# Neighbourhood attention layer on one core: last pair split into an output operand, bias rows held once, weight tiles freed singly, last row scaled on two engines

## The chip, the cores and the metric

The kernel runs on one core of a Trainium2 chip. The metric is the device time in microseconds of one execution, taken as the median of several runs. The core has a matrix engine (TensorE, in the profile PE, with its weight loads as PEld), three engines for elementwise work (VectorE or DVE, ScalarE or ACT, GpSimd or POOL) and SyncE (SP), which here issues all the transfers between HBM and the on-chip memory SBUF. Products go to eight PSUM banks. Each engine runs its own instructions in order and waits for others through semaphores.

## The reference

One layer of an encoder: RMSNorm, one projection to q, k, v and a gate, two-dimensional neighbourhood attention (16 heads of 64, a grid of 32 rows by 64 columns, windows of 8 rows by 16 columns, a learned bias per head), a SiLU gate, an output projection with a residual, and a last RMSNorm. x is (1, 2048, 1024) in float32.

```python
def neighbourhood_mixer(h, w_in, rpb):
    proj = h @ w_in
    q, k, v, gate = jnp.split(proj, 4, axis=-1)
    o = neighbourhood_attention(heads(q), heads(k), heads(v), rpb)
    return o.reshape(B, S, D_INNER), gate
...
    s = jnp.einsum('bnqhd,bknjhd->bhnqkj', qr, kr) * scale
    s = jnp.where(col_valid, s + bias, NEG_INF)
    p = jax.nn.softmax(s, axis=-1)
    o = jnp.einsum('bhnqkj,bknjhd->bnqhd', p, vr)
...
h = rmsnorm(x, g)
o, gate = neighbourhood_mixer(h, w_in, rpb)
x = x + (o * jax.nn.silu(gate)) @ w_out
return rmsnorm(x, norm_f)
```

## The kernel before

Each float32 operand of a large product is split into two parts that the matrix engine takes at full rate, a high one (ACT rounds it) and a low one (DVE or POOL subtracts the high one from the value). A product of 128x128 by 128x512 is then three matmuls: high by high, high by low, low by high.

The program is written out by hand in one order per engine. Its main parts are these.

The start warms PE with ten matmuls of zeros (L780). `first_groups` (L417) then multiplies the first k weight tile by the first quarter of x as its pieces come in, `load_item` having issued all the loads on SP.

`projections` (L430) is a generator that yields after every matmul. It runs over 56 "halves", each a unit of q, k, v or gate for one quarter of the rows. `items` lists what has to be loaded and split, in order; `load_ahead` issues the loads (L151 for weights into tiles called raw), and `consume` calls `use_item`, which splits one item (L197 on ACT, L198 on DVE or POOL). `may_use` (L272) holds a weight item back while five weight tiles are live; a tile is live until the whole half that uses it last is done. `group` (L378) multiplies q, k and gate units, `group_v` (L394) V units. `evac` (L348) takes a product from PSUM, scales it by the row norms and writes q, k (split) and gate to scratch tensors in HBM.

The attention runs over 64 steps `pairs[i]`: two heads (a pair p of eight), a group T of eight grid rows (four of them, called row groups), and two of four column blocks C. For one step, `scores` multiplies (L549) and adds the bias tables em on DVE (L556) ahead of an exponential on ACT; `normalise` (L562) has the reciprocals on DVE and scales x on POOL (L567); `turns` transposes x through PE (L572) and copies it to pta on DVE and ACT (L596, L597); `values` multiplies by V (L617), and after the second step of a pair og is gated on DVE (L631) and stored to the scratch tensor ogd (L634). The bias tables of a pair come from its raw bias rows e (two tiles, L519): `bias` (L523) adds a mask, one on POOL and one on DVE for each column type. Pairs run p = 0 to 7 in row group 0, then six pairs in row groups 1, 2, 3 each, and the last two pairs interleaved.

The loop at L852 interleaves all this: for each step it feeds a fixed number of matmuls of `projections` (later of `outputs`) by a clock that counts them, with `normalise` and `turns` of the step before and `scores` of the step itself between them. `store(key, lag, f)` puts an action off by so many counts of that clock, and loads for the next step go the same way (`later_loads`).

`outputs` (L726) multiplies the 16 row tiles of 128 rows by the two halves of the output weights. `load_og` (L655) loads a row tile of ogd (512 KB, eight pairs) once all its pairs are stored, `split_og` (L665) splits it on ACT and DVE. `add_rows` adds the residual, `finish` (L692) computes the norm on DVE, scales the two halves of the row tile and sends them.

The lines that decide the waits in question:

```python
live = {tiles_(*i[1:]) for i in items[:state["used"]] if i[0] == "w" and last_use["w", i[1]] >= d}
return len(live | {tiles_(a, b)}) <= 5
...
ep = pool("ep", 4)
...
later_loads(load_qk(*nx), 5, 4)
if nx[0] != p:
    later_loads(load_e(nx[0]), 20, 3)
```

Of the kernel before, what the change touches and what calls it, by code (L numbers as in the profile page):

```python
# [67 lines left out]
def build(ctx, tc, x, xt, wg, rpb, w_out, n0, nf, masks, out):  # L68
# [25 lines left out]
    mp = pool("mp", 6)  # L94
    ep = pool("ep", 4)
    ev = pool("ev", 8)
# [33 lines left out]
    raws, wh, wl, asked_at = {}, {}, {}, {}  # L130
    woh, wol = {}, {}

    def load_item(it):
# [12 lines left out]
        asked_at[it] = clock[0]  # L146
        if kind in "xs":
            nc.sync.dma_start(t, xt[a * 128:(a + 1) * 128, b * 512:(b + 1) * 512])
        elif kind == "w":
            u = a[0]  # L150
            nc.sync.dma_start(t.rearrange("p (k c) -> p k c", c=256), wg[u, :, 2 * b:2 * b + 2, :])  # L151
        else:
            nc.sync.dma_start(t, w_out[a * 128:(a + 1) * 128, b * 512:(b + 1) * 512])
# [10 lines left out]
    def use_item(it):  # L164
# [7 lines left out]
        if kind == "x":  # L172
# [4 lines left out]
            if b < 2:  # L177
                raws["z", a, b] = t
        elif kind in "sz":
            square(a, t, b)  # L180
        elif kind == "w":
# [9 lines left out]
            else:  # L191
# [4 lines left out]
                h, l = wh[a, b // 2][:, s], wl[a, b // 2][:, s]  # L196
            nc.scalar.activation(h, t, AF.Copy)  # L197
            (nc.gpsimd if (b + u) % 2 and state["half"] > 0 else nc.vector).tensor_tensor(l, t, h.bitcast(F32), OP.subtract)  # L198
        else:
# [68 lines left out]
    AHEAD = 5  # L268
    clock = [0.0]
    state = dict(used=0, loaded=0, half=-1, done_halves=0, event=0.0)  # L270
# [107 lines left out]
    def group(w, a, c, n):  # L378
        p = bank(512, "pp")
        cols = slice(a * 128, a * 128 + 128)  # L380
        for k in range(NK):
# [7 lines left out]
            yield 1  # L389
            nc.tensor.matmul(p, wl[w, k // 4][:, k % 4, cols], hh[k, c], start=False, stop=(k == NK - 1))  # L390
            yield 1
        return p

    def group_v(w, t):  # L394
# [3 lines left out]
        for k in range(NK):  # L398
# [6 lines left out]
            yield 1  # L405
            nc.tensor.matmul(p, hl[k, c][:, o], h, start=False, stop=(k == NK - 1))  # L406
            yield 1
            if k in (2, 5):
# [8 lines left out]
    def first_groups(w):  # L417
        ps = [bank(512, "pp") for _ in range(2)]
        for k in range(NK):
            need(("x", k, 0))  # L420
            need(("w", w, k // 2))
            for a, p in enumerate(ps):
                cols = slice(a * 128, a * 128 + 128)
                h, l = wh[w, k // 4][:, k % 4, cols], wl[w, k // 4][:, k % 4, cols]
                nc.tensor.matmul(p, h, hh[k, 0], start=(k == 0), stop=False)
                nc.tensor.matmul(p, h, hl[k, 0], start=False, stop=False)
                nc.tensor.matmul(p, l, hh[k, 0], start=False, stop=(k == NK - 1))
        return ps

    def projections():  # L430
        for n, (kind, j, ph, c) in enumerate(halves):
# [10 lines left out]
            else:  # L442
                for a in range(2):
# [4 lines left out]
                    if n == len(halves) - 1:  # L448
# [3 lines left out]
                        else:  # L452
                            split_og(0)
                    if n >= 4:
# [15 lines left out]
    KT, VT, QT, EM, SG, E = {}, {}, {}, {}, {}, {}  # L470
    OG = {}
# [131 lines left out]
    def values(i):  # L603
# [25 lines left out]
        if cs[1] == 3:  # L629
# [3 lines left out]
            def keep():  # L633
                nc.sync.dma_start(ogd[T][:, :, p], og.rearrange("p (i q) -> p i q", i=4))  # L634
                written.add(("og", p, T))

            store(("og", p, T), 4, keep)

# [11 lines left out]
    tiles = S // 128  # L650

    def og_ready(n):
        return all(("og", p, n // 4) in written for p in range(NP))

    def load_og(n):  # L655
        T, i = divmod(n, 4)
        must(*[("og", p, T) for p in range(NP)])
        G[n] = t = wp([128, NK, 128], F32, "ograw")
        nc.sync.dma_start(t, ogd[T][:, i])

# [4 lines left out]
    def split_og(n):  # L665
# [3 lines left out]
        for j in range(2):  # L669
            s = slice(4 * j, 4 * j + 4)  # L670
            nc.scalar.activation(h[:, s], t[:, s], AF.Copy)  # L671
            nc.vector.tensor_tensor(l[:, s], t[:, s], h[:, s].bitcast(F32), OP.subtract)  # L672
        G[n] = (h, l)

    squared = [0]

    def add_rows(n, j, ps):
# [8 lines left out]
        def square():  # L686
            nc.scalar.activation(xr, y, AF.Square, scale=0.5 ** 0.5, accum_out=st[:, j:j + 1])
            squared[0] += 1

        store(("y", n, j), 5, square)  # L690

    def finish(n):  # L692
        y, st = Y.pop(n)
        h, r, a = st[:, 2:3], st[:, 3:4], st[:, 4:5]
# [9 lines left out]
        def scale():  # L704
            nc.vector.scalar_tensor_tensor(y[0], y[0], r, late["nf"][0], op0=OP.mult, op1=OP.mult)
            if n == tiles - 1:
                nc.vector.scalar_tensor_tensor(y[1], y[1], r, late["nf"][1], op0=OP.mult, op1=OP.mult)
            else:
                nc.scalar.activation(y[1], y[1], AF.Copy, scale=r)
# [16 lines left out]
    def outputs():  # L726
# [19 lines left out]
        for k, (n, j) in enumerate(turns_):  # L746
# [7 lines left out]
            gh, gl = G[n]  # L754
            p = bank(512, "po")
            for i in range(NK):
                while (i, j) not in woh:
                    consume(1, True)
                if k < 6 and i % 2 == 0:
                    consume(1)  # L760
                nc.tensor.matmul(p, gh[:, i], woh[i, j], start=(i == 0), stop=False)  # L761
                yield 1
                nc.tensor.matmul(p, gl[:, i], woh[i, j], start=False, stop=False)  # L763
                yield 1
                nc.tensor.matmul(p, gh[:, i], wol[i, j], start=False, stop=(i == NK - 1))  # L765
                yield 1
# [11 lines left out]
    zp = bank(512, "zp")  # L778
    for _ in range(10):
        nc.tensor.matmul(zp, z[:, :128], z, start=True, stop=True)  # L780
# [39 lines left out]
    def prepare(i):  # L820
# [85 lines left out]
```

## Time and profile before

| | us |
|---|---|
| median of three runs | 1155.54 (1155.35 to 1156.7) |
| the profiled execution | 1155.26 |
| its span, first to last instruction | 1153.5 |
| PE busy in the span | 1125.1 |
| mean granted clock of PE | 0.993 of full |
| HBM read and written | 155.91 MB and 67.11 MB |

The profile is one execution. Busy time of PE is the union of its matmuls, whose ends overlap: a matmul of 512 columns is listed with 0.39 us, but two follow each other at 0.227 us from start to start. What counts for PE is therefore the time from start to start. A row of the timeline gives start, duration, engine, line of the kernel, operation and tiles, and in brackets the idle time of that engine just before it with what ended it. "SPq" rows are the issuing of transfers by SP, not the transfers; a DMA row in the chain of waits is the time from the issue to the release of what waited.

### The profile page before, as it was taken

How to read it: one execution, taken by the hardware profiler on the slowest of the kernel's cores; microseconds unless marked ns; L12 is line 12 of the kernel's file. 1: busy time of each engine (PE TensorE's matmuls, PEld its weight loads, DVE VectorE, ACT ScalarE, POOL GpSimd, SP SyncE). 2: the span in 40 equal slices, each digit the busy share in tenths (PEclk: the TensorE clock that was granted, in tenths of full speed). 3: DMA queues.
4: the chain of work that ended last, by engine and by line, in shares of the span. 5: the costliest groups of instructions: out<-in, count | busy, mean ns of one | idle time of the engine just before them, and what ended most of it. 6: DMA issues, size and time to landing. Idle time of an engine off the chain costs nothing.

```text
span 1153.5 us, 21778 instructions
## 1 busy us (share of the span) xinstructions
PE 1125.1 (98%) x7858; PEld 916.4 (79%) x7858; DVE 572.6 (50%) x1453; ACT 467.5 (41%) x1190; POOL 383.7 (33%) x461
## 2 busy tenths in 40 slices
PE   8989999999999999999999999999999999999997
PEld 6868888888788888878887788888778777788875
DVE  6620554441244564126565455346555756566544
ACT  8222344232333444234444454344444544444322
POOL 1210442432232143314443544225533553233300
PEclk9999999999999999999999999999999999999999
DMA  7453867564554678457686787658877975865352
GB/s 244 126 160 109 270 213 219 162 225 110 154 183 145 214 222 240 118 165 195 224 245 198 207 250 222 208 163 230 235 230 210 281 230 188 255 194 189 104 174 73
DMA packets 139755, 224.45 MB, mean 195 GB/s; under 512 B 11776, under 2 KB 56320, under 8 KB 139648
## 3 DMA queue, kind: packets, MB, share of 16 engines
q1 hardware_dynamic: 139648, 223.06, 63.7%
q8 instruction: 62, 1.02, 0.4%
q14 instruction: 45, 0.37, 0.1%
HBM read 155.91 MB, written 67.11 MB: 193 GB/s over the span
## 4 chain that ended last, share of the span: by engine, by line
PE 58%; DMA 6%; DVE 3%; issue 3%; POOL 3%; ACT 1%; SPq 0%; DVEq 0%; POOLq 0%; ACTq 0%
PE pp L390 9%; PE pp L386 8%; PE pp L388 8%; PE o L617 6%; PE s L549 5%; PE po L763 4%; PE po L765 4%; PE po L761 4%; PE ph L572 3%; PE pv L404 3%; PE pv L402 3%; PE pv L406 3%; POOL x L567 1%; DMA ograw<-ogd 1%; DMA ogd<-og 1%
## 5 line engine op out<-in xcount | busy, mean ns | idle before, releaser
L390 PE MATMUL pp<-hh,wl 128*128 128x512 f32 x752 | 296.3, 394 | 2.0 <-POOL wl L198 2.0
L386 PE MATMUL pp<-hh,wh 128*128 128x512 f32 x752 | 295.3, 393 | 0.0
L388 PE MATMUL pp<-hl,wh 128*128 128x512 f32 x752 | 293.9, 391 | 0.0
L567 POOL TENSOR_SCALAR x<-x,st 128x360 f32<-128x360 f32 (+5 forms) x256 | 154.6, 623 | 250.7 <-DVE st L565 226.4
L559 ACT ACTIVATE x<-x,st 128x360 f32<-128x360 f32 (+5 forms) x256 | 151.8, 594 | 49.4 <-DVE st L556 49.3
L390 PEld LDWEIGHTS pp<-hh,wl 128*128 128x128 f32 x752 | 141.1, 188 | 33.4 <-POOL wl L198 2.9
L388 PEld LDWEIGHTS pp<-hl,wh 128*128 128x128 f32 x752 | 141.2, 188 | 30.5 <-issue 0.7
L386 PEld LDWEIGHTS pp<-hh,wh 128*128 128x128 f32 x752 | 141.2, 188 | 29.5 <-issue 0.5
L597 DVE COPY pta<-ph 128x384 f32<-128x384 f32 (+3 forms) x128 | 61.3, 516 | 165.8 <-PE ph L572 165.7
L198 POOL TENSOR_TENSOR wl<-raw,wh 128x512 fp32r<-128x512 f32 x60 | 83.3, 1393 | 161.6 <-ACT wh L197 155.2
L556 DVE CUSTOM_DVE_ANT_0 x<-s,em 128x360 f32<-128x360 f32 (+5 forms) x256 | 123.9, 539 | 7.3 <-PE s L549 5.3
L198 DVE TENSOR_TENSOR wl<-raw,wh 128x512 fp32r<-128x512 f32 x64 | 61.4, 969 | 93.9 <-ACT wh L197 92.6
L596 ACT ACTIVATE pta<-ph 96x256 f32<-96x256 f32 (+1 forms) x224 | 59.2, 333 | 118.7 <-PE ph L572 118.7
L402 PE MATMUL pv<-wh,hh 128*128 128x512 f32 x256 | 100.9, 394 | 3.5 <-ACT wh L197 3.5
L761 PE MATMUL po<-woh,gh 128*128 128x512 f32 x256 | 100.4, 392 | 2.1 <-ACT gh L671 2.0
L404 PE MATMUL pv<-wl,hh 128*128 128x512 f32 x256 | 101.4, 396 | 1.0 <-DVE wl L198 1.0
L763 PE MATMUL po<-woh,gl 128*128 128x512 f32 x256 | 100.4, 392 | 1.6 <-DVE gl L672 1.6
L765 PE MATMUL po<-wol,gh 128*128 128x512 f32 x256 | 100.9, 394 | 0.0
L406 PE MATMUL pv<-wh,hl 128*128 128x512 f32 x256 | 100.4, 392 | 0.0
L617 PEld LDWEIGHTS o<-pta,vt 96*64 96x64 f32 (+2 forms) x1792 | 83.8, 137 | 16.4 <-issue 11.0
L549 PE MATMUL s<-kt,qt 64*128 64x360 f32 (+5 forms) x768 | 93.1, 356 | 2.2 <-DVE pta L597 1.9
L531 POOL TENSOR_TENSOR em<-e,mk 128x360 f32<-128x360 f32 (+5 forms) x75 | 65.0, 869 | 89.9 <-DVE st L556 80.4
(85 smaller groups left out, 1373.9 us busy)
## 6 DMA issues: line engine op xcount, KB each, us to landing
raw<-in_wg_dram SPq DMA_DIRECT2D x124, 256.0 KB
vt<-vd SPq DMA_DIRECT2D x64, 192.0 KB
raw<-in_xt_dram SPq DMA_DIRECT2D x36, 256.0 KB
e<-in_rpb_dram SPq DMA_DIRECT2D x36, 240.0 KB
k_hi<-hi SPq DMA_DIRECT2D x32, 256.0 KB
k_lo<-lo SPq DMA_DIRECT2D x32, 256.0 KB
q_hi<-hi SPq DMA_DIRECT2D x32, 256.0 KB
q_lo<-lo SPq DMA_DIRECT2D x32, 256.0 KB
```

The costliest lines, as they stand in the source:

```text
L198: (nc.gpsimd if (b + u) % 2 and state["half"] > 0 else nc.vector).tensor_tensor(l, t, h.bitcast(F32), OP.subtract)
L386: nc.tensor.matmul(p, wh[w, k // 4][:, k % 4, cols], hh[k, c], start=(k == 0), stop=False)
L388: nc.tensor.matmul(p, wh[w, k // 4][:, k % 4, cols], hl[k, c], start=False, stop=False)
L390: nc.tensor.matmul(p, wl[w, k // 4][:, k % 4, cols], hh[k, c], start=False, stop=(k == NK - 1))
L404: nc.tensor.matmul(p, hh[k, c][:, o], l, start=False, stop=False)
L549: nc.tensor.matmul(pst[s], qq[a, qs], kk[a, :r1 - r0, c0:c1], start=(m == 0), stop=(m == 2))
L559: nc.scalar.activation(X[i, C][s], X[i, C][s], AF.Exp, bias=st[:, s:s + 1], scale=-1.0, accum_out=st[:, 2 + s:3 + s])
L567: nc.gpsimd.tensor_scalar(X[i, C][s], X[i, C][s], st[:, 4 + s:5 + s], 0.5, op0=OP.mult, op1=OP.mult)
L617: nc.tensor.matmul(o[s * 64:s * 64 + 64, C * 128 + q0:C * 128 + q0 + nq], vt[C][:k, g - g0_, s * 64:s * 64 + 64], t[:k, at:at + nq], start ...
L761: nc.tensor.matmul(p, gh[:, i], woh[i, j], start=(i == 0), stop=False)
L763: nc.tensor.matmul(p, gl[:, i], woh[i, j], start=False, stop=False)
L765: nc.tensor.matmul(p, gh[:, i], wol[i, j], start=False, stop=(i == NK - 1))
```

## The change

It has these parts.

Weight tiles are freed singly: `group` and `group_v` add a tile to `freed` after the last matmul that reads it, and `may_use` leaves freed tiles out. The first weight tile is loaded and split in two halves, `first_groups` takes each of the three products for both column halves of the unit before it takes the next, and 21 warming matmuls stand in place of 10.

Bias rows have two buffers in place of four; their load moves from the first step of a pair (lag 20) to the second (lag 3, ahead of the gate's load).

The last pair of each of the row groups 1, 2 and 3 is split from SBUF right after its gating, for the first two row tiles of the group, into a pool of its own. Its slot in ogd is the last one, and the loads of those two row tiles leave it out. The loads wait until a store is at least 12 counts old. The split of row tile 0 is put off by 9 counts.

In the last row tile the gain vector is multiplied in on DVE beforehand, one half is then scaled by ACT and the other by DVE, and the first half is sent from ACT's queue.

```diff
-    ep = pool("ep", 4)
+    ep = pool("ep", 2)
+    lp = pool("lp", 2)
...
+            if it == items[1]:
+                nc.sync.dma_start(raws[items[0]][:, 256:], wg[items[0][1][0], :, 1, :])
...
+            if it == items[0]:
+                nc.sync.dma_start(t[:, :256], wg[u, :, 0, :])
...
-            nc.scalar.activation(h, t, AF.Copy)
-            (nc.gpsimd if (b + u) % 2 and state["half"] > 0 else nc.vector).tensor_tensor(l, t, h.bitcast(F32), OP.subtract)
+            def part(s, e):
+                nc.scalar.activation(h[:, s], t[:, s], AF.Copy)
+                e.tensor_tensor(l[:, s], t[:, s], h[:, s].bitcast(F32), OP.subtract)
+            if it == items[0]:
+                part(slice(0, 1), nc.vector)
+                second.append(lambda: part(slice(1, 2), nc.vector))
+            else:
+                part(slice(0, 2), nc.gpsimd if (b + u) % 2 and state["half"] > 0 else nc.vector)
...
-            live = {tiles_(*i[1:]) for i in items[:state["used"]] if i[0] == "w" and last_use["w", i[1]] >= d}
+            live = {tiles_(*i[1:]) for i in items[:state["used"]] if i[0] == "w" and last_use["w", i[1]] >= d} - freed
...
+            if k % 4 == 3 and a == 1 and n == last_use["w", w]:
+                freed.add((*w, k // 4))
...
+            if k % 2 and t % 4 == 3 and state["half"] == last_use["w", w]:
+                freed.add((*w, k // 2))
...
-                h, l = wh[w, k // 4][:, k % 4, cols], wl[w, k // 4][:, k % 4, cols]
-                nc.tensor.matmul(p, h, hh[k, 0], start=(k == 0), stop=False)
-                nc.tensor.matmul(p, h, hl[k, 0], start=False, stop=False)
-                nc.tensor.matmul(p, l, hh[k, 0], start=False, stop=(k == NK - 1))
+            for m in range(3):
+                for a, p in enumerate(ps):
+                    t = (wl if m == 2 else wh)[w, k // 4][:, k % 4, cols]
+                    nc.tensor.matmul(p, t, (hl if m == 1 else hh)[k, 0], start=(k == 0 and m == 0),
+                                     stop=(k == NK - 1 and m == 2))
...
-                            split_og(0)
+                            store(("og0",), 9, lambda: split_og(0))
...
+    lastp = {T: p for p, T in order}
+    def slot(T, p):
+        return 7 if p == lastp[T] else p - (p > lastp[T])
...
+            def direct():
+                h, l = lp([128, 256], F32R, "lh"), lp([128, 256], F32R, "ll")
+                LAST[T] = h, l
+                nc.scalar.activation(h, og[:, :256], AF.Copy)
+                nc.vector.tensor_tensor(l, og[:, :256], h.bitcast(F32), OP.subtract)
+            if T and p == lastp[T]:
+                store(("last", T), 2, direct)
             store(("og", p, T), 4, keep)
...
+    def parts(n):
+        T, i = divmod(n, 4)
+        return NK - 1 if T and i < 2 else NK
...
+        return all(("og", p, T) in written and clock[0] - stored_at[p, T] >= 12 for p in range(NP)
+                   if slot(T, p) < parts(n)) and (parts(n) == NK or T in LAST)
...
-        nc.sync.dma_start(t, ogd[T][:, i])
+        nc.sync.dma_start(t[:, :parts(n)], ogd[T][:, i, :parts(n)])
...
+            if n == tiles - 1:
+                w = (raw if j else ev)([128, 512], F32, "yw")
+                nc.vector.tensor_tensor(w, y, late["nf"][j], OP.mult)
+                Y[n][0][j] = w
...
-            nc.vector.scalar_tensor_tensor(y[0], y[0], r, late["nf"][0], op0=OP.mult, op1=OP.mult)
             if n == tiles - 1:
-                nc.vector.scalar_tensor_tensor(y[1], y[1], r, late["nf"][1], op0=OP.mult, op1=OP.mult)
+                nc.scalar.activation(y[0], y[0], AF.Copy, scale=r)
+                nc.vector.tensor_scalar(y[1], y[1], r, None, op0=OP.mult)
...
-                nc.sync.dma_start(out[n * 128:n * 128 + 128, 512 * j:512 * j + 512], y[j])
+                (nc.scalar if n == tiles - 1 and j == 0 else nc.sync).dma_start(
+                    out[n * 128:n * 128 + 128, 512 * j:512 * j + 512], y[j])
...
-    for _ in range(10):
+    for _ in range(21):
         nc.tensor.matmul(zp, z[:, :128], z, start=True, stop=True)
...
-                if nx[0] != p:
-                    later_loads(load_e(nx[0]), 20, 3)
         else:
-            later_loads([lambda: load_sg(p, T)], 6, 0)
+            if nx and nx[0] != p:
+                later_loads(load_e(nx[0]), 3, 2)
+            later_loads([lambda: load_sg(p, T)], 7, 0)
```

More of the change, by code (lines that the diff above doesn't have):

```diff
@@ L131, in build @@
     woh, wol = {}, {}
+    second = []
     def load_item(it):
@@ L178, in use_item @@
                 raws["z", a, b] = t
+            if it == items[1]:
+                second.pop()()
         elif kind in "sz":
@@ L269, in build @@
     clock = [0.0]
+    freed = set()
     state = dict(used=0, loaded=0, half=-1, done_halves=0, event=0.0)
@@ L633, in keep @@
             def keep():
-                nc.sync.dma_start(ogd[T][:, :, p], og.rearrange("p (i q) -> p i q", i=4))
+                nc.sync.dma_start(ogd[T][:, :, slot(T, p)], og.rearrange("p (i q) -> p i q", i=4))
                 written.add(("og", p, T))
+                stored_at[p, T] = clock[0]
+            def direct():
[5 more added lines that the diff above has]
+                store(("last", T), 2, direct)
             store(("og", p, T), 4, keep)
@@ L650, in build @@
     tiles = S // 128
+    def parts(n):
+        T, i = divmod(n, 4)
+        return NK - 1 if T and i < 2 else NK
     def og_ready(n):
-        return all(("og", p, n // 4) in written for p in range(NP))
+        T = n // 4
+        return all(("og", p, T) in written and clock[0] - stored_at[p, T] >= 12 for p in range(NP)
+                   if slot(T, p) < parts(n)) and (parts(n) == NK or T in LAST)
     def load_og(n):
         T, i = divmod(n, 4)
-        must(*[("og", p, T) for p in range(NP)])
+        must(*[("og", p, T) for p in range(NP) if slot(T, p) < parts(n)])
         G[n] = t = wp([128, NK, 128], F32, "ograw")
-        nc.sync.dma_start(t, ogd[T][:, i])
+        nc.sync.dma_start(t[:, :parts(n)], ogd[T][:, i, :parts(n)])
     def load_res(n, j):
@@ L669, in split_og @@
         for j in range(2):
-            s = slice(4 * j, 4 * j + 4)
+            s = slice(4 * j, min(4 * j + 4, parts(n)))
             nc.scalar.activation(h[:, s], t[:, s], AF.Copy)
             nc.vector.tensor_tensor(l[:, s], t[:, s], h[:, s].bitcast(F32), OP.subtract)
-        G[n] = (h, l)
+        G[n] = [(h[:, i], l[:, i]) for i in range(parts(n))]
+        if parts(n) < NK:
+            q = slice(n % 4 * 128, n % 4 * 128 + 128)
+            G[n].append((LAST[n // 4][0][:, q], LAST[n // 4][1][:, q]))
     squared = [0]
@@ L753, in outputs @@
                 ready["split"] += 1
-            gh, gl = G[n]
             p = bank(512, "po")
+            who = {slot(n // 4, q): q for q in range(NP)}
             for i in range(NK):
-                while (i, j) not in woh:
+                gh, gl = G[n][i]
+                q = who[i]
+                while (q, j) not in woh:
                     consume(1, True)
```

17 lines of the change are left out of this document (9 added, 8 removed).

## The prediction

> **What bounds the kernel now.** I read the page first, then the windows, then PE's waits, and last the timeline round each wait. The page's row of each engine gives busy time, share and instructions:
>
> ```profile
> span 1153.5 us, 21778 instructions
> PE 1125.1 (98%) x7858; PEld 916.4 (79%) x7858; DVE 572.6 (50%) x1453; ACT 467.5 (41%) x1190; POOL 383.7 (33%) x461
> ```
>
> TensorE is the bound: 28.4 us of 1153.5 are left in which it does nothing, so no rearrangement gains more than that plus what PE loses while its clock is halved. The windows say where those gaps lie (columns: stretch, length, busy time and instructions of PE, PEld, DVE, ACT, POOL, granted clock, DMA share, GB/s):
>
> ```profile
> 0.00:21.00 21.00, 16.61 (x59) 11.56 (x60) 12.67 (x18) 15.52 (x25) 4.14 (x9) 0.92 0.88 305
> 57.00:75.00 18.00, 13.57 (x51) 10.39 (x50) 6.87 (x8) 5.92 (x11) 5.10 (x4) 0.91 0.78 232
> ...
> 525.00:900.00 375.00, 371.63 (x3295) 303.12 (x3292) 204.21 (x559) 174.14 (x492) 152.98 (x202) 1.00 0.74 219
> 900.00:1000.00 100.00, 94.33 (x788) 75.28 (x787) 63.81 (x176) 48.71 (x136) 48.23 (x58) 0.98 0.75 224
> ...
> 1145.70:1153.50 7.80, 0.00 (x0) 0.00 (x0) 3.76 (x12) 0.72 (x2) 0.00 (x0) 0.67 0.18 67
> ```
>
> Idle are 4.4 us at the start, 4.4 round 61 us, 3.4 from 525 to 900, 5.7 from 900 to 1000, and 7.8 after the last matmul. The first two stretches also show a granted clock under 1. PE's waits name the releasers (total us, times, longest):
>
> ```profile
> PE pv L402 <- ACT wh L197: 3.5, 1, 3.5
> PE ph L572 <- POOL x L567: 3.2, 12, 0.4
> PE pp L425 <- ACT hh L175: 2.3, 1, 2.3
> PE pp L390 <- POOL wl L198: 2.0, 2, 1.0
> PE po L761 <- ACT gh L671: 2.0, 2, 1.7
> PE s L549 <- DVE pta L597: 1.9, 2, 1.2
> ...
> PE po L763 <- DVE gl L672: 1.6, 4, 0.9
> PE pv L404 <- DVE wl L198: 1.0, 1, 1.0
> ```
>
> Nearly every row belongs to a place that the diff touches. I take them in order of time.
>
> **Start (21 warming matmuls, first weight tile in halves, order of the first products).**
>
> ```profile
> 1.83 3.81 PE L780 MATMUL zp<-z 128*128 128x512 bf16 x10 [1.83 <-POOL z L777]
> 7.91 0.50 PE L425 MATMUL pp<-hh,wh 128*128 128x512 f32 x1 [2.27 <-ACT hh L175]
> ...
> 10.57 0.63 PE L427 MATMUL pp<-hh,wl 128*128 128x512 f32 x1
> 11.00 0.63 PE L425 MATMUL pp<-hh,wh 128*128 128x512 f32 x1
> ...
> 20.64 0.39 PE L427 MATMUL pp<-hh,wl 128*128 128x512 f32 x1
> 20.87 0.39 PE L386 MATMUL pp<-hh,wh 128*128 128x512 f32 x1
> ```
>
> Ten warming matmuls end at 5.64, PE stands still until 7.91, and then starts at half speed (0.43 us from start to start); at 20.64 it is 0.227. The first 48 products end at 20.87. The slow part after the restart ends soon after 11.00, some 3.5 us on; after the stall at 61 us (below) it ends at about 69.5, 4.6 us after its restart. So with 21 warming matmuls and no pause I estimate that the clock opens 3.5 to 4.6 us after 1.83: 8 to 11 of them at 0.43, the rest at 0.227, and the first product at 8.2 to 8.8. The halved weight tile brings its data earlier, not later, than 7.91, and the added ACT, DVE and DMA instruction each lie under that. 48 x 0.227 = 10.9, so the products end at 19.1 to 19.7: **gain 1.4**. If the clock did not open by then: 1.83 + 21 x 0.43 = 10.9, 3.5 us more at half speed, and an end at 23.4: a loss of 2.5.
>
> The Trainium skill speaks against my 3.5 to 4.6: "TensorE: Matmul & The Clock Gate", section "Part 1: The HAM clock gate (the "warmup" mystery)", has the gate judged over free-running windows of about 3.4 us, so that the opening depends on where a window happens to lie. By that the clock opens 3.4 to 6.8 us after 1.83, the warming matmuls end at 8.2 to 9.8, and the gain is 0.2 to 1.8 us, differing from run to run.
>
> **The wait at 61 us (weight tiles freed singly).**
>
> ```profile
> 61.10 0.39 PE L406 MATMUL pv<-wh,hl 128*128 128x512 f32 x1
> 64.94 0.50 PE L402 MATMUL pv<-wh,hh 128*128 128x512 f32 x1 [3.46 <-ACT wh L197]
> ...
> 69.86 0.40 PE L402 MATMUL pv<-wh,hh 128*128 128x512 f32 x1
> ...
> 48.25 5.80 SPq L151 DMA_DIRECT2D raw<-in_wg_dram  x4
> 53.72 4.76 SPq L151 DMA_DIRECT2D raw<-in_wg_dram  x4
> ...
> 54.25 1.23 ACT L197 ACTIVATE wh<-raw 128x512 fp32r<-128x512 f32 x2 [2.89 <-DMA raw<-in_wg_dram]
> ```
>
> From 61.10 to 69.86 PE starts ten matmuls: 8.76 us against 2.27 at full speed, so the wait and the halved clock behind it cost 6.5. The cause is the order: the fourth tile of V may be split only when the last q half is done, so its ACT and DVE instructions stand behind four evacuations, and the built program has only 9 matmuls between the second of its splits and the first use. After the change the first q tile is free after half of the last group: 27 matmuls, and the splits stand ahead of the evacuations. What is late next is the raw tile. The load issued at 48.25 was used at 54.25, 6.0 us later; the tile in question is issued at 53.72 and so lands near 59.7, and ACT (0.6) and DVE (0.7) make it ready at 61.0, against a need at 61.3. That is tight, and the evacuations queue behind it on ACT and DVE, where PSUM has spare banks. **Gain 6.2**, between 4 (the load 2 us later, a pause too short to halve the clock) and 6.5.
>
> The same edit moves the other late splits from 9 to 18 or 24 matmuls ahead of their use. The two waits of L390 on POOL's wl are 1.0 each and 15 more matmuls are 3.4 us: **gain 2.0**, at worst 1.
>
> **The same releases reorder DVE and POOL before 900 us; the first output split moves.**
>
> ```profile
> 815.76 1.77 DVE L198 TENSOR_TENSOR wl<-raw,wh 128x512 fp32r<-128x512 f32 x1 [1.22 <-ACT wh L197]
> ...
> 903.12 1.82 DVE L672 TENSOR_TENSOR gl<-ograw,gh 128x512 fp32r<-128x512 f32 x2
> ```
>
> The first stands just ahead of copies of pta that PE waits for; in the built program it now stands before that evacuation. The second is the split of row tile 0, now issued nine steps later, behind those copies. Together they are the two waits of L549: 1.9. Of the 3.2 us that L572 waits for POOL's x, one case goes (a wl of POOL moves ahead) and another gets a wl in front: I take 0.6, between -1 and 3.2. **Gain 2.5.**
>
> **Last pair split straight from SBUF.**
>
> ```profile
> 975.98 3.13 DMA ogd<-og
> 979.13 5.04 DMA ograw<-ogd
> ```
>
> In the chain of waits, the load of the next row group waits 3.1 us for the store of the last pair, then takes 5.0. After the change the first two loads leave the last slot out and no longer wait for that store (in the built program they have no such semaphore); they are issued behind it on SP, 2.6 us earlier. That covers the longest wait of L761 on gh (1.7). Three row groups have this step; their waits are what L761 and L763 show, 2.0 + 1.6, less the 0.9 of L763 that belongs to row tile 2. **Gain 2.7**, at most 3.6. The added splits of a half tile (one ACT, one DVE) stand behind og in the shadow of the next pair; without that cover they would cost 0.7 each time.
>
> **Last row on two engines.**
>
> ```profile
> 1138.29 0.72 ACT L709 ACTIVATE y<-y,st 128x512 f32<-128x512 f32 x1 [2.06 <-DVE st L702]
> ...
> 1149.17 0.75 DVE L705 SCALAR_TENSOR_TENSOR y<-y,st,acc 128x512 f32<-128x512 f32 x1
> 1149.84 0.74 DVE L707 SCALAR_TENSOR_TENSOR y<-y,st,acc 128x512 f32<-128x512 f32 x1
> ```
>
> The two DVE rows end at 1150.58. Now ACT scales one half (0.72) while DVE scales the other, both from 1149.2, ending at 1149.9: **gain 0.7**. The products with the gain vector move ahead, under ACT's square. A store issued by ACT is in no row; I take it as SP's.
>
> **Bias rows held once: the cost.** Two buffers instead of four put each load of e behind the last use of the old rows, in the second half of a pair instead of the first.
>
> ```profile
> 926.75 3.37 SPq L519 DMA_DIRECT2D e<-in_rpb_dram  x2
> 935.67 1.82 SPq L507 DMA_DIRECT2D vt<-vd  x2
> ...
> 938.87 1.93 POOL L531 TENSOR_TENSOR em<-e,mk 128x360 f32<-128x360 f32 x2 [2.18 <-DMA e<-in_rpb_dram]
> 942.68 2.40 POOL L567 TENSOR_SCALAR x<-x,st 128x480 f32<-128x480 f32 x4 [1.88 <-DVE st L565]
> ...
> 948.15 0.92 PE L572 MATMUL ph<-ident,x 64*128 64x64 f32 x24
> ...
> POOL em L531 <- DMA e<-in_rpb_dram: 9.4, 2, 7.3
> ```
>
> Here the rows took 12.1 us from 926.75 and POOL already waited for them. They will now be issued behind the vt loads, at about 937.5. What waits behind em on POOL is x (2.40), and PE turns x at 948.15, so they must be there at 948.15 - 2.40 - 1.93 = 943.8, 6.3 us after the issue. At the 6.0 of the raw tile this costs nothing, at 12.1 it costs 5.8; between the two I take 2.5. The other seven changes of pair after 525 us showed no such wait before (two in all, the other at the first use), and I give them 0.5 together, between 0 and 6. **Cost 3.0**, between 0 and 12. Before 525 us the distance is twice as long.
>
> **The sum.** 1.4 + 6.2 + 2.0 + 2.5 + 2.7 + 0.7 = 15.5, less 3.0, is 12.5. The profiled execution took 1155.26 (span 1153.5 and 1.76 round it), 0.3 under the median 1155.54. 1155.3 - 12.5 = **1142.8 us**.
>
> **The rivals.**
> 1. Slower: the bias rows become the bound. All eight changes lie in a stretch with a DMA share of 0.74, POOL and DVE are in order, and em blocks x and the reciprocals behind it. It decides once the eight delays together exceed the 15.5 gained, 2 us at each; at 2.5 each the time is 1155.3 - 15.5 + 20 = 1159.8. For it speaks the 12.1 us above, against it that no other change waited.
> 2. The gaps after 525 us move instead of going: PE reaches POOL's x and the splits sooner, and the 5.2 of the two parts there return as other waits. 1142.8 + 5.2 = 1148.0. For it: L572 has 12 short waits, so POOL runs just behind PE; against it: the named instructions leave the place.
> 3. The release does not do what it says: the raw tile lands after 63, and ACT and DVE, blocked by it, hold the evacuations too. Most of 6.2 stays: 1148.5.
> 4. The clock stays half open until the products run: 1.4 turns into -2.5, 1146.7. For it: ten matmuls from 1.83 to 5.64 did not open it; against it: both restarts opened it within 4.6 us.
>
> **Chances.** Forecast 0.60 (1139 to 1146), rival 1 0.06, rival 2 0.18, rival 3 0.08, rival 4 0.08. The best sum of the bounds is 1.7 + 6.5 + 2.0 + 5.1 + 3.6 + 0.7 = 19.6 without a cost, 1135.7; the range goes from there to where rivals 2 and 3 and half the cost of the rows add up: 1135 to 1150. The measurement tells 0.2% (2.3 us) from no change. Faster 0.92 (all but rival 1 and a part of its neighbourhood), same 0.02, slower 0.06.
>
> **What would show it.** After the change PE's waits have no row of L402 on ACT's wh and none of pp on POOL's wl; the granted clock is below 1 only in the first 9 us; the first group ends at 19 to 20 us; the loads of ograw for the first two tiles of a row group leave within 1 us of the store before them; about 2.9 us lie between the last scaling and the end, as now. Wrong would be: waits of em on e that sum to over 10 us with PE idle behind them, or a wait of the V product on a raw tile of over 3 us.

## The result

| | before | after |
|---|---|---|
| median of the runs side by side, us | 1156.07 (1153.76 to 1156.7) | 1145.65 (1144.62 to 1147.82) |
| the profiled execution, us | 1155.26 | 1146.7 |
| its span, us | 1153.5 | 1144.9 |

The ratio is 0.9914, with a 95% interval of 0.9901 to 0.9927: faster, by 10.4 us in the medians and 8.6 between the two profiled executions. The forecast was 12.5 and 1142.8.

The page of the kernel after, the row of the engines:

```profile
span 1144.9 us, 21822 instructions
PE 1124.5 (98%) x7869; PEld 918.0 (80%) x7869; DVE 578.9 (51%) x1458; ACT 470.9 (41%) x1195; POOL 385.9 (34%) x461
```

PE's work is the same (11 warming matmuls more); its idle time went from 28.4 to 20.4 us. The windows of after, with the same columns as before (stretch, length, then PE, PEld, DVE, ACT, POOL, granted clock, DMA share, GB/s):

```profile
0.00:21.00 21.00, 19.17 (x74) 12.72 (x75) 12.98 (x20) 16.01 (x27) 4.10 (x9) 1.00 0.89 306
57.00:75.00 18.00, 18.00 (x81) 14.87 (x80) 6.48 (x8) 6.17 (x11) 4.67 (x4) 1.00 0.78 244
...
525.00:900.00 375.00, 372.09 (x3307) 303.21 (x3306) 211.39 (x562) 175.18 (x493) 153.95 (x204) 1.00 0.74 220
900.00:1000.00 100.00, 92.12 (x772) 73.87 (x771) 65.28 (x170) 48.16 (x135) 44.16 (x51) 0.97 0.68 203
1000.00:1137.15 137.15, 137.15 (x864) 112.70 (x863) 76.80 (x229) 50.86 (x133) 35.81 (x41) 1.00 0.52 164
1137.15:1144.90 7.75, 0.00 (x0) 0.00 (x0) 3.52 (x12) 1.45 (x3) 0.00 (x0) 0.72 0.18 68
```

From 57 to 75 PE runs 81 matmuls in place of 51 and is never idle. From 900 to 1000 it is worse off than before: 7.9 us idle in place of 5.7, and a clock of 0.97. PE's waits (total us, times, longest) name what is left:

```profile
PE ph L598 <- POOL x L593: 7.9, 16, 3.2
PE zp L832 <- POOL z L829: 1.8, 1, 1.8
PE po L813 <- ACT gh L712: 1.6, 1, 1.6
PE po L815 <- DVE gl L713: 0.9, 1, 0.9
PE s L575 <- ACT pta L622: 0.3, 1, 0.3
```

The wait on POOL's x grew from 3.2 to 7.9, and its longest from 0.4 to 3.2. POOL's and DVE's waits tell why:

```profile
POOL em L557 <- DMA e<-in_rpb_dram: 56.7, 14, 10.4
...
DVE em L557 <- DMA e<-in_rpb_dram: 20.7, 9, 6.9
```

Before, POOL waited 9.4 us for the bias rows e and DVE never; now it is 77 in sum.

A table of positions tells where time was won and lost. It gives the start of the first score product of a step (counted from 0) and of the last output matmul, from the timelines. A step that starts earlier than in another kernel has won that much by then; at the steps shown all kernels have run the same products.

```
step          before    after  bias_only  freed_only  e_first  no_direct
1             168.38   161.00     168.41      162.02   160.16     161.22
20            580.23   570.01     580.19      571.05   569.19     570.27
50            903.21   892.94     905.46      892.67   890.78     893.34
51            917.79   905.86     919.99      907.21   903.70     906.26
53            937.61   927.15     939.83      927.14   925.75     929.39
55            960.97   956.27     967.94      950.34   948.93     957.31
56            972.21   967.71     977.92      961.81   958.92     967.30
57            989.03   982.11     996.82      980.18   973.47     987.85
63           1075.72  1068.30    1083.00     1066.37  1059.65    1074.04
last matmul  1145.23  1136.76    1152.39     1135.85  1128.12    1143.38
```

Before minus after: 7.4 at step 1, 10.2 at step 20, still 10.3 at step 50, 11.9 at 51, 10.5 at 53, only 4.7 at 55, 6.9 at 57, 8.5 at the last matmul, 8.6 at the end of the span. So more than the final gain was won by 570 us; 5.8 were lost again between 927 and 956, and 3.8 came back behind that. The columns are one execution each. tail_sp and tail_one (below) run the same program as the changed kernel up to the last row tile, and their positions differ from its by up to 1.1 us.

### The profile page after: what moved, and what is told of

Its sections match the earlier page's. It is cut to its first block, busy times and chain, and to the rows that moved or that the text cites. A ratio compares the mean times of both kernels' runs of the same rounds, so it can differ in the third digit from the quotient of the medians.

```text
span 1144.9 us, 21822 instructions
## 1 busy us (share of the span) xinstructions
PE 1124.5 (98%) x7869; PEld 918.0 (80%) x7869; DVE 578.9 (51%) x1458; ACT 470.9 (41%) x1195; POOL 385.9 (34%) x461
## 4 chain that ended last, share of the span: by engine, by line
PE 85%; DMA 6%; POOL 3%; issue 2%; DVE 2%; ACT 1%; SPq 0%; POOLq 0%; DVEq 0%; ACTq 0%
PE pp L408 13%; PE pp L406 13%; PE pp L404 13%; PE o L643 6%; PE s L575 6%; PE pv L424 5%; PE pv L422 5%; PE pv L426 5%; PE po L817 4%; PE po L813 4%; PE po L815 4%; PE ph L598 4%; POOL x L593 2%; DMA vt<-vd 2%; DMA sgt<-sgd 1%
## 5 line engine op out<-in xcount | busy, mean ns | idle before, releaser
L209 POOL TENSOR_TENSOR wl<-raw,wh 128x512 fp32r<-128x512 f32 x60 | 80.2, 1340 | 224.5 <-ACT wh L208 217.7
L557 POOL TENSOR_TENSOR em<-e,mk 128x360 f32<-128x360 f32 (+5 forms) x75 | 67.9, 911 | 121.7 <-DVE st L582 61.4
L209 DVE TENSOR_TENSOR wl<-raw,wh 128x512 fp32r<-128x512 f32 (+1 forms) x65 | 59.3, 916 | 78.9 <-ACT wh L208 78.6
L813 PE MATMUL po<-woh,gh 128*128 128x512 f32 x244 | 95.5, 391 | 1.6 <-ACT gh L712 1.6
L815 PE MATMUL po<-woh,gl 128*128 128x512 f32 x244 | 95.4, 391 | 0.9 <-DVE gl L713 0.9
L817 PE MATMUL po<-wol,gh 128*128 128x512 f32 x244 | 96.2, 394 | 0.0
```

Of the source, the lines that this page charges most:

```text
L813: nc.tensor.matmul(p, gh, woh[q, j], start=(i == 0), stop=False)
L817: nc.tensor.matmul(p, gh, wol[q, j], start=False, stop=(i == NK - 1))
```

## The experiments

Each ratio is to the kernel before, run on the same chip. Times are medians, in us.

**The bias rows alone, put on the kernel before (bias_only).**

```diff
-    ep = pool("ep", 4)
+    ep = pool("ep", 2)
...
-                if nx[0] != p:
-                    later_loads(load_e(nx[0]), 20, 3)
...
-            later_loads([lambda: load_sg(p, T)], 6, 0)
+            if nx and nx[0] != p:
+                later_loads(load_e(nx[0]), 3, 2)
+            later_loads([lambda: load_sg(p, T)], 7, 0)
```

> The kernel before with the edit of the bias rows alone: two buffers for e instead of four, its load in the second step of a pair at lag 3 instead of the first at lag 20. Theory A (the late bias rows hold em, and em holds x on POOL, at the changes of pair after 525 us): 6 at the change near 940 us, as between the two profiles, and 2 to 5 spread over the other seven: 1163 to 1167 us against 1156, and POOL's and DVE's waits of em on e rise from 9 us to 60 or more. Theory B (those gaps come from POOL's order, shifted by the freed tiles, and would be there with the rows early): within 1 us of before. My prediction's own term was 3.0, so 1159.

Measured 1161.47 against 1156.69, ratio 1.0045 (1.0031 to 1.0059): 5.2 slower by the ratio, between the two theories' figures but on A's side. The waits of PE and of POOL:

```profile
PE ph L572 <- POOL x L567: 7.7, 18, 2.5
...
POOL em L531 <- DMA e<-in_rpb_dram: 60.9, 10, 13.8
```

Nearly the 7.9 of the changed kernel, without any freed tile. In the table of positions it loses 2.3 by step 50 and 4.8 more from step 53 to 55, the place where the changed kernel loses 5.8. Theory B falls.

**The freed weight tiles alone (freed_only).**

```diff
+    freed = set()
...
-if i[0] == "w" and last_use["w", i[1]] >= d}
+if i[0] == "w" and last_use["w", i[1]] >= d} - freed
...
+            if k % 4 == 3 and a == 1 and n == last_use["w", w]:
+                freed.add((*w, k // 4))
...
+            if k % 2 and t % 4 == 3 and state["half"] == last_use["w", w]:
+                freed.add((*w, k // 2))
```

> The kernel before with nothing but the weight tiles freed singly. By the terms of the prediction 6.2 at 61 us and 2.0 at the two waits on POOL's wl, and 1 to 2 for the wl split that stood ahead of pta at 816 us: 1146 to 1148 us. By the reading of the two profiles (6.5 and 2.8 before 525 us, nothing net after it because waits on POOL's x return elsewhere): 1146 to 1147, with waits of the transposes on x of 3 to 5 us in sum. If the release by itself also brings the new waits on x of the changed kernel: about 8 us of them, 1149 to 1151.

Measured 1145.54, ratio 0.9904 (0.9882 to 0.9926): as fast as the whole change, and a little under the 1146 to 1148 expected. Its waits on x:

```profile
PE ph L577 <- POOL x L572: 2.8, 10, 0.4
...
POOL em L536 <- DMA e<-in_rpb_dram: 6.0, 3, 3.4
```

So the release of the tiles neither brings the waits on x nor takes them away: 2.8 where 3.2 had been. The rest of the change adds up to nothing: what it wins, the bias rows take.

**The bias rows earlier in the changed kernel (e_early, e_first).** In e_early the load follows the last use of the old rows in the pair's first step:

```diff
-            if nx and nx[0] != p:
-                later_loads(load_e(nx[0]), 3, 2)
...
             tables(i)
+            if i % 2 == 0 and i + 2 < N and pairs[i + 2][0] != pairs[i][0]:
+                later_loads(load_e(pairs[i + 2][0]), 10, 2)
```

> The changed kernel with the load of the bias rows put off from the first step's last use of the old rows by only 10 counts, so still two buffers, but some 25 counts and two vt loads earlier than in the changed kernel. Theory A: PE's waits on POOL's x fall from 7.9 to about 3 us, the 3.2 us wait near 941 us and the halved clock behind it go: 5 to 8 us less, 1138 to 1141. Theory B: the waits on x stay between 6 and 9 us, 1145 to 1147.

In e_first it stays in the second step but goes ahead of that step's loads of vt:

```diff
+        change = cs[0] and nx and nx[0] != p
+        if change:
+            later_loads(load_e(nx[0]), 0, 2)
-        later_loads([lambda C=C: load_v(p, T, C) for C in cs], 0, 2)
+        later_loads([lambda C=C: load_v(p, T, C) for C in cs], 4 if change else 0, 2)
...
-                later_loads(load_e(nx[0]), 3, 2)
```

> The changed kernel with the bias rows still loaded in the second step, but ahead of that step's two vt loads instead of behind them: 3 counts and two transfers earlier, about 3 us. Theory A: the loads of 9 to 10 us that made PE wait 3.2 near 941 us end in time or nearly: 1140 to 1144. If only the latency under the load of transfers counts and not the place behind vt: above 1144. Theory B: 1145 to 1147.

Measured 1141.01 for e_early, ratio 0.9861 (0.984 to 0.9883), and 1139.14 for e_first, 0.9849 (0.9827 to 0.9872). e_early is at the edge of its range, e_first under its own. A second time e_first had 1139.54 and 0.9861 (0.9845 to 0.9878):

> The kernel with the bias rows ahead of the vt loads once more, beside the next one on the same chip: 1138 to 1140, ratio to before 0.983 to 0.987.

Both bring PE's waits on x back to 2.8. For e_first:

```profile
PE ph L598 <- POOL x L593: 2.8, 10, 0.4
PE po L813 <- ACT gh L712: 2.4, 1, 2.4
```

So two buffers are enough; it was the place of the load that cost. The change near 940 us shows how, first in the changed kernel (SP's issues, POOL and PE from its timeline: start, duration, engine, line, tiles, in brackets the idle time ahead):

```profile
923.64 1.28 SPq L533 DMA_DIRECT2D vt<-vd  x2
925.23 0.55 SPq L660 DMA_DIRECT2D ogd<-og  x1
926.40 2.51 SPq L545 DMA_DIRECT2D e<-in_rpb_dram  x2
...
936.66 2.21 POOL L557 TENSOR_TENSOR em<-e,mk 128x360 f32<-128x360 f32 x2 [10.45 <-DMA e<-in_rpb_dram]
940.23 2.38 POOL L593 TENSOR_SCALAR x<-x,st 128x480 f32<-128x480 f32 x4 [1.36 <-DVE st L591]
...
940.95 0.28 PE L598 MATMUL ph<-ident,x 64*128 64x64 f32 x2 [3.20 <-POOL x L593]
...
943.20 2.44 PE L575 MATMUL s<-kt,qt 64*128 64x360 f32 x12
```

and in e_first:

```profile
922.24 0.81 SPq L545 DMA_DIRECT2D e<-in_rpb_dram  x2
...
925.07 1.28 SPq L533 DMA_DIRECT2D vt<-vd  x2
...
928.93 2.23 POOL L557 TENSOR_TENSOR em<-e,mk 128x360 f32<-128x360 f32 x2 [4.12 <-DMA e<-in_rpb_dram]
932.52 2.39 POOL L593 TENSOR_SCALAR x<-x,st 128x480 f32<-128x480 f32 x4 [1.37 <-DVE st L591]
...
937.00 1.52 PE L575 MATMUL s<-kt,qt 64*128 64x360 f32 x12
```

Ahead of vt the rows are issued 4.2 us earlier and take 6.7 us to POOL's start in place of 10.3, so x is there 7.7 us earlier; 1.4 of that is the lead which e_first already has at step 53. Behind vt, em is late, x stands behind em, PE waits 3.2 us, and then takes 2.44 us for its twelve score products in place of 1.52, at a granted clock of 0.50 (943.0 to 945.6 us). That e_early isn't better than e_first though its load is earlier is seen in one wait: its longest on gh is 3.3, behind which its granted clock from 900 to 925 is 0.86, in e_first 1.00. These too are single executions: in the profile of e_first's second run that wait is 2.6 and the clock 0.93.

**The last pair from SBUF taken out (no_direct).**

```diff
-    lp = pool("lp", 2)
...
-            if T and p == lastp[T]:
-                store(("last", T), 2, direct)
...
-        return NK - 1 if T and i < 2 else NK
+        return NK
...
-        return all(("og", p, T) in written and clock[0] - stored_at[p, T] >= 12 for p in range(NP)
-                   if slot(T, p) < parts(n)) and (parts(n) == NK or T in LAST)
+        return all(("og", p, T) in written for p in range(NP)
+                   if slot(T, p) < parts(n))
```

> The changed kernel without the part on the last pair: no split from SBUF, no pool for it, all eight slots loaded from ogd, loads as soon as the stores are issued. Theory: the chain store, load, split comes back at the ends of the row groups, by the rows of the kernel with the freed tiles alone 2.8 us near 980 (gh and gl) and 0.9 near 1097: 3.5 to 4 us more than the changed kernel, 1149 to 1150; the prediction's term was 2.7, at most 3.6. Rival: the waits there were covered by the later PE after the late bias rows, so that nothing is lost: 1145 to 1146.

Measured 1150.99, ratio 0.9959 (0.9946 to 0.9973): 5.2 more than the changed kernel by the ratios, 0.9959 against 0.9914, more than expected. The edit takes out two things at once, the split from SBUF and the 12 counts that a store must be old; no run tells them apart. PE's waits between 975 and 990 us, and the window of that stretch:

```profile
PE po L804 <- ACT gh L703: 2.7, 1, 2.7
...
975.00:990.00 15.00, 12.34 (x82) 9.18 (x82) 5.66 (x17) 3.23 (x9) 1.41 (x3) 0.77 0.84 258
```

The chain of store, load and split returns, as a wait of 2.7 with the clock at 0.77 round it. In the changed kernel PE waits for nothing there, and the load leaves 0.05 us behind the end of the store's issue (972.04):

```profile
971.48 0.56 SPq L660 DMA_DIRECT2D ogd<-og  x1
972.09 0.89 SPq L700 DMA_DIRECT2D ograw<-ogd  x1
```

**The split of row tile 0 not put off (og0_now).**

```diff
-                            store(("og0",), 9, lambda: split_og(0))
+                            split_og(0)
```

> The changed kernel with the split of row tile 0 where it was, without the 9 counts. Theory (the gain of the delay is given back at once): the copy of pta is 1.2 to 1.6 us late again near 894 us, but the split of row tile 2, which waits on ACT behind the last output weights from HBM near 915, makes PE wait 1.2 to 1.6 us less there, so that by 930 us both kernels stand within 0.3 us of each other. Rival (the prediction's term holds): PE stays 1.5 us behind.

One execution, 1145.54. The score products of step 51 start at 907.54, 1.7 later than in the changed kernel; the first output matmul of row tile 2 waits less (0.7 on gh in place of 1.6), yet at step 53 the kernel is still 1.5 behind (928.62 against 927.15), and only the wait for the late bias rows takes that away: step 54 starts at 943.23 against 943.20. So the gain was given back, but 15 us later than I had expected, and what hid it was the wait on e, not the wait on the weights. PE's timeline shows why the weights did not:

```profile
916.25 0.49 PE L813 MATMUL po<-woh,gh 128*128 128x512 f32 x1 [0.69 <-ACT gh L712]
917.64 0.50 PE L815 MATMUL po<-woh,gl 128*128 128x512 f32 x1 [0.90 <-DVE gl L713]
...
918.22 0.61 PE L813 MATMUL po<-woh,gh 128*128 128x512 f32 x1
918.63 0.63 PE L815 MATMUL po<-woh,gl 128*128 128x512 f32 x1
```

Two short waits were enough to halve the clock (0.41 from start to start).

**The last two stores (tail_sp, tail_one).** tail_sp sends both halves from SP:

```diff
-            for j in range(2):
-                (nc.scalar if n == tiles - 1 and j == 0 else nc.sync).dma_start(
-                    out[n * 128:n * 128 + 128, 512 * j:512 * j + 512], y[j])
+            for j in ((1, 0) if n == tiles - 1 else (0, 1)):
+                nc.sync.dma_start(out[n * 128:n * 128 + 128, 512 * j:512 * j + 512], y[j])
```

> The changed kernel with both halves of the last row tile sent from SP, the DVE half first, instead of one from ACT. Theory (a store issued by ACT costs more): from the end of the later scaling to the end of the span 2.9 to 3.1 us as with the kernels that send from SP, against 3.5 with ACT's store. Rival (the last half is late since both stores leave together): 3.4 to 3.6.

One execution, 1146.29, span 1144.5. The end of its timeline:

```profile
1140.29 0.72 ACT L754 ACTIVATE yw<-yw,st 128x512 f32<-128x512 f32 x1 [2.00 <-DVE st L750]
1140.30 0.49 DVE L755 TENSOR_SCALAR yw<-yw,st 128x512 f32<-128x512 f32 x1
1140.81 0.81 SPq L763 DMA_DIRECT2D out_dram<-yw  x2
```

The later scaling ends at 1141.01, the span 3.5 later, as with ACT's store (changed kernel: 1141.41 and 1144.9): my theory fell, the rival held. tail_one then sends one half only:

```diff
-            for j in range(2):
+            for j in range(1 if n == tiles - 1 else 2):
```

> The changed kernel with only the ACT half of the last row tile sent, from ACT's queue; the other half of that row tile is not written. Theory (the two stores share the transfer, so the end comes some 3.6 us after the first of them starts, whoever issues the second): from the end of ACT's scaling to the end of the span 2.5 to 2.9 us. Rival (a store issued by ACT takes longer in itself): 3.4 to 3.6, as with both.

One execution, span 1143.4:

```profile
1139.79 0.72 ACT L754 ACTIVATE yw<-yw,st 128x512 f32<-128x512 f32 x1 [2.00 <-DVE st L750]
...
1140.55 0.37 ACTq L763 DMA_DIRECT2D out_dram<-yw  x1
```

From 1140.51 to the end 2.9 us. ACT's store by itself is no slower. Two stores that are issued 0.24 us (changed kernel) or 0.42 us (tail_sp) apart end 3.5 us behind the later scaling, and 3.7 behind the first issue in both; in before, where the scalings and the two issues are 0.66 apart, it is 2.9 (1150.58 to 1153.5).

**Fewer warming matmuls and the stores from SP, on e_first (best).**

```diff
-    for _ in range(21):
+    for _ in range(15):
```

and the diff of tail_sp.

> The changed kernel with the bias rows ahead of the vt loads, 15 warming matmuls in place of 21, and both last stores from SP, the DVE half first. From 1139.1 of the bias rows ahead: 0.5 to 1.3 less at the start (six matmuls, at full rate 0.23 each, as far as the first split x is there at 7.2 to 7.9) and 0.5 less at the end: 1137 to 1138. Rival for the start: with fewer matmuls the clock is not open at the first products more often, and the time spreads more or is 1 to 2 us longer.

Measured 1140.03, ratio 0.9866 (0.9849 to 0.9884): no better than e_first, and over the expected 1137 to 1138. The first product starts at 7.78, 0.3 earlier than in e_first's profile, and PE then waits 3.3 on gh near 914 in place of 2.4: PE is there 0.3 earlier, and ACT has the weights from HBM 0.6 later (913.54 in place of 912.90). The stores from SP gain nothing, from the last matmul's end to the end of the span it is 7.8 us in both. The clock opened only with the first product (below); fewer warming matmuls than 15 were not tried.

**The output weights one tile further ahead, on e_first (ahead6).**

```diff
-        while state["loaded"] < min(len(items), max(state["used"] + AHEAD, 32)):
+        while state["loaded"] < min(len(items), max(state["used"] + (6 if items[min(state["used"], len(items) - 1)][0] == "o" else AHEAD), 32)):
```

> The changed kernel with the bias rows ahead of the vt loads, and the output weights loaded six tiles ahead instead of five. Theory (what every kernel here loses near 914 us is the last output weight's way from HBM: ACT waits for it with the split of row tile 2 behind): the wait of the first matmul on gh falls from 2.4 us to under 1, 1136 to 1138 us. Rival (the transfers there are held by the load on HBM, or the load waits on SP for the tile to come free, so that it lands no earlier): no change, 1139 to 1141.

Measured 1137.23, ratio 0.9845 (0.9822 to 0.9868). In its profile the wait on gh near 914 us is gone. The kernel stands 3.5 ahead of e_first's profile from there on, until a wait of 1.0 on gh near 968, for the next row group, takes 1.8 of it back. Both were then run beside each other:

> The same with the output weights six tiles ahead, once more. If the 1.7 us between the two profiles are lasting, 1.5 to 2 us less than the kernel beside it; if the wait for the row group's last store near 968 us gives all of it back in the mean, within 0.5 us.

1136.5 and 0.9836 (0.9822 to 0.9851), against 1139.54 for e_first: 3 us, lasting, and more than the 1.5 to 2 expected. Of all kernels tried it is the fastest, 9 us faster than the changed one. PE's waits in that second profile:

```profile
PE ph L598 <- POOL x L593: 3.1, 11, 0.4
PE zp L832 <- POOL z L829: 1.8, 1, 1.8
PE po L815 <- DVE gl L713: 1.5, 2, 1.3
PE o L643 <- DVE pta L623: 0.5, 1, 0.5
PE po L813 <- ACT gh L712: 0.3, 1, 0.3
```

The 1.3 on gl is what is left of the wait near 914 in that execution.

## Why the prediction was right, and where it was off

The forecast 1142.8 was 2.9 under the median of 1145.65, inside the range. By the table of positions the terms came out so (gains in us between the two profiled executions, whose difference is 8.6):

| term | forecast | measured | from |
|---|---|---|---|
| start | 1.4 | 0.9 | first product behind the group: 20.87 to 20.00 |
| wait at 61 us | 6.2 | 6.5 | 7.4 at step 1, less 0.9 |
| waits on POOL's wl | 2.0 | 2.8 | step 1 to 20 |
| reorder, first output split | 2.5 | 1.6 | 1.4 to step 50, 1.7 at 51, less 1.5 given back at 53 |
| last pair from SBUF | 2.7 | 4.0 | step 56 (4.5 ahead) to the last matmul (8.5) |
| last row | 0.7 | 0.1 | 8.5 at the last matmul, 8.6 at the end |
| bias rows | -3.0 | -7.3 | -1.3 to step 50, -6.0 from 53 to 56 |

The six gains add up to 15.9 where 15.5 was forecast, but single ones missed by up to 1.3 both ways and the misses cancel: that the sum of the gains is right is in part luck. The cost is not; it missed by 4.3, and the range was wide enough for it. The terms are differences of single executions. From step 53 to 56, the changed kernel loses 6.0 on before, tail_sp 5.8 and tail_one 4.2, so a row of the table stands to 1 or 2 us.

The 1.3 of the bias rows before step 50 is a difference of two kernels: e_first stands 2.2 ahead of the changed kernel there, 0.8 of it from the start. The 1.4 beside it is what remains of the 0.05 that the stretch from step 20 to 50 won in all.

- **The wait at 61 us and the waits on wl** were right in cause and nearly in size; freed_only shows that this edit alone makes the whole measured gain. Rival 3 (a late raw tile) didn't happen: from 57 to 75 PE is never idle.
- **The bias rows** are the term that was mis-sized, by 4.3 in this execution; by the ratios the rows cost 5.2 in bias_only, and their load ahead of vt gains 6 to 7.5 in the changed kernel, against the forecast 3.0. The mechanism, the place and the need were right (issue behind vt, x behind em, about 6.3 us of room). I took 2.5 for it, between 0 at the raw tile's 6.0 us and 5.8 at the 12.1 that this very load had taken before. It took 10.3, and PE lost the 4 us of lateness and then more, since the clock halved behind it. Nor are there eight changes of pair after 525 us: the trace of before has nine loads of the rows there, from 578 to 1029. The row of the same transfer at the same place should have weighed more than that of another one. The sign that was named as proof of the contrary, waits of em on e over 10 us with PE idle behind, is what the profile shows, for this term: 77 us of such waits, and 7.9 of PE on x.
- **Rival 1** (the rows become the bound) didn't decide: one change of pair took most of the cost. Between 525 and 900 us PE's single waits on x stay at 0.6 and below:

```profile
PE ph L598 <- POOL x L593: 2.8, 9, 0.6
```

- **Rival 2** (gaps move) had one true instance, at the split of row tile 2. The copies of pta no longer hold PE, but PE then waits earlier for the output weights and the bias rows (og0_now). The waits on x did not move by themselves; freed_only has 2.8 of them.
- **The last pair** was undersized by 1.3, and its loss without it is 5.2. The sum of the waits was right for before; for an earlier PE the wait is longer, and it halves the clock. The loads leave right behind the store, as forecast. That the granted clock would be under 1 in the first 9 us alone was wrong for the same reason as the term of the rows: 0.97 from 900 to 1000.
- **The last row** was right on the engines: from the last matmul's end to the end of the later scaling 4.26 us after (1137.15 to 1141.41) and 4.96 before, 0.7. But the span ended 3.5 behind the scaling and not 2.9, since the two stores left nearly together. Showing it needed the runs with both stores on SP and with one store.

By the Trainium skill, "DMA: Bandwidth & Descriptors", section "Issuing engines are not separate DMA queues", transfers started by different engines run on the same 16 DMA engines and interleave. The tail agrees: with ACT and SP or with SP alone the end comes 3.5 us behind the scaling, with one store 2.9.

- **The start** won less than 1.4 in this execution, because the clock opened later than I took it to (5.5 us after the first matmul, below). Rival 4 did not come true: the clock was open at the first product. Its reason against the change, that ten warming matmuls had not opened it, was a misreading, as these windows of before show:

```profile
1.80:4.60 2.80, 2.77 (x7) 1.04 (x8) 0.00 (x0) 0.21 (x1) 0.00 (x0) 1.00 0.56 110
4.60:5.70 1.10, 1.04 (x4) 0.23 (x2) 0.00 (x0) 0.23 (x1) 0.00 (x0) 1.00 0.76 171
5.70:7.90 2.20, 0.00 (x0) 0.00 (x0) 0.70 (x2) 1.16 (x3) 0.00 (x0) 1.00 1.00 370
7.90:10.90 3.00, 2.71 (x6) 2.00 (x7) 3.00 (x5) 2.97 (x5) 0.00 (x0) 0.56 1.05 396
```

Seven matmuls in 2.8 us, then four in 1.1 (one of the ten is counted in both rows): the rate had gone up, and it was gone again after the pause of 2.3 us (the granted clock 0.56 behind it). The granted clock reads 1.00 in the first row too, where the matmuls run at half rate; at the start of the program the distance from start to start has to tell.

## What to carry to other kernels

Fewer buffers for a tile move its load behind the last use of the old one; then ask what stands ahead of that load on its queue, and order the queue by what is needed first: here two buffers were enough once the rows went ahead of vt. Price a transfer that becomes just in time by its own slowest row, not by another transfer's, and add what PE loses at half clock behind the wait. A wait that is removed ahead of a transfer with a fixed arrival is given back at that transfer, so look for the next arrival before counting the gain.

## What the runs showed that was not expected

The same 21 warming matmuls end at different times. The first product starts at 7.92 (tail_one), 8.07 (e_first), 8.92 (after) and 9.14 (no_direct). By the starts of the warming matmuls, 0.43 us apart until the clock opens and 0.22 behind, it opened 3.4, 3.8, 5.5 and 6.0 us after the first one at 1.83; in before 3.0, in best 5.9. My 3.5 to 4.6 was too narrow. By the Trainium skill, "TensorE: Matmul & The Clock Gate", section "Part 1: The HAM clock gate (the "warmup" mystery)", the windows are free-running and some 3.4 us long. If the opening falls one to two windows after the first matmul, an estimate worked out from that page, it comes 3.4 to 6.8 us after it; the spread agrees with that, save for the 3.0. The Trainium skill's own figure there, around 4 us give or take 0.5, does not cover what was measured here.

The clock closed after short pauses: after 2.3 us at the start of before (0.56 behind it), after 2.7 in no_direct (0.77 from 975 to 990), and after 0.69 and 0.90 within some 2 us in og0_now (0.56 from 918 to 920). In e_first a wait of 2.4 did not close it. All these pauses are shorter than the window of some 3.4 us that the Trainium skill gives there. A wait of 1 to 3 us may thus cost its own length or a few microseconds more; what decides between the two, no run here shows.
